# Row sums of squares on TensorE: one 128 by 128 identity per step, or two 64 by 64 identities on the diagonal of the array

## The chip, the core and the metric

The kernel runs on one core of a Trainium2 chip. The core has TensorE (matmuls; PE in the profile, its weight loads PEld), VectorE (DVE), ScalarE (ACT), GpSimd (POOL), SyncE (SP, which only issues DMAs here), an on-chip memory SBUF with 128 partitions, and PSUM, the accumulators that TensorE writes, eight banks in each partition. The metric is the time of one execution on the device in microseconds. Three runs of the kernel before gave 193.05, 191.87 and 192.48 us; the median is 192.48.

## The reference

Cosine-similarity attention for 8 batches of 12 heads, 512 positions, 64 numbers per position:

```python
Q_norm = Q / (np.linalg.norm(Q, axis=-1, keepdims=True) + 1e-10)
K_norm = K / (np.linalg.norm(K, axis=-1, keepdims=True) + 1e-10)
scores = np.einsum('bhqd,bhkd->bhqk', Q_norm, K_norm) / tau          # tau = 0.1
weights = np.exp(scores - np.max(scores, axis=-1, keepdims=True))
weights = weights / (np.sum(weights, axis=-1, keepdims=True) + 1e-10)
return np.einsum('bhqk,bhkd->bhqd', weights, V).astype(np.float32)
```

For each of the 96 heads: a norm for each of 512 rows of Q and of K, 512 by 512 scores, their exponentials, and the weighted sum of V.

## The kernel before

The heads are worked through in 48 pairs, s = 0 to 47. A pair goes through these steps; the names in brackets are those of the program's own order tables.

- **Load** (LD, LV; line 429 and 432): Q and K of a pair into `qk`, V into `vf`.
- **Squares** (SQ, line 250): POOL squares Q and K of the pair into `sq`, 128 partitions of 16 rows of 64 numbers, in bf16.
- **Sums of squares** (SSQ, lines 266 to 271): each of the 16 rows has 64 numbers to be added up. TensorE does the first part. Eight matmuls with the identity matrix `ident` as stationary operand each read 16 rows by 8 numbers (128 columns) and are accumulated in the same 128 columns of PSUM, so that 64 numbers of a row become 8. The changed lines are these. The result lies in bank "x" (and in banks "o1" and "o0" for pairs 1 and 2).
- **Reduce** (RED, line 276): DVE adds up the remaining 8.
- **Norms** (NEW, lines 390 to 402): DVE works out 1/sqrt in a few Newton steps, for groups of one or two pairs.
- **Scale** (SCL, line 296): DVE scales Q, POOL scales K, into `qn`.
- **Transpose** (TR, line 484): 16 matmuls for a pair, each on 64 of the 128 rows of the array (the two halves in turn, written to two banks of PSUM), and a DVE copy (EVA, line 490) into `qt`. For seven pairs K goes through a DMA instead.
- **Scores** (SCO, line 512): four chunks for each pair. A chunk is two matmuls, one for each head, on 64 rows of the array each, 512 columns, into two banks of `scps`. There are two such pairs of banks, used in turn, so a chunk may start when the exponentials of the chunk two before it have been read.
- **Exponentials** (EXP, line 527): ACT reads a chunk, 128 by 1024, and writes `et`. There are 184 such instructions on line 527 and a few others at both ends.
- **Weighted sums** (PV, line 543): 32 matmuls for a pair, each on all 128 rows and columns of the array, 65 columns wide, in eight pieces of four.
- **Normalise and store** (RCP line 557, NRM line 559, ST line 563).

The order of the work is a table written out by hand for each engine (`ORDER`); an engine runs its list in order and waits on semaphores where an operation needs another's result. In TensorE's list each SSQ stands between two other operations. Of the 47 SSQs, 29 stand between two SCOs; 9 come after a PV and before an SCO, 4 after an SCO and before a PV, 2 between two PVs, 2 between an SCO and a TR, 1 between a TR and an SCO. So an SSQ touches a PV on 9 + 4 + 2 x 2 = 17 sides. (One of the two transposes beside an SSQ, that of pair 1 on line 301, uses all 128 rows and columns too; it runs at 11.5 us, before the steady part.)

On the array's shapes, as the profile's rows write them: `64*128` is a matmul on 64 rows and 128 columns of the array (SCO, TR), `128*128` one on the whole array (SSQ, PV), and `128*64` one on 64 columns only (the 16 transposes of pair 0, line 333).

Of the kernel before, what the change touches and what calls it, by code (L numbers as in the profile page):

```python
# [124 lines left out]
def bass_cosine_similarity_attention_kernel(  # L125
# [16 lines left out]
    R_QK, R_V, R_SQ, R_QN, R_QT, R_ET, R_O = 18, 6, 6, 5, 5, 3, 8  # L142
# [3 lines left out]
    def sb(name, shape, dt):  # L146
        return nc.alloc_sbuf_tensor(name, shape, dt)
# [4 lines left out]
    sq = [sb(f"sq{i}", [128, 16, DIM], bf16) for i in range(R_SQ)]  # L152
# [13 lines left out]
    ident = sb("ident", [128, 128], bf16)  # L166
# [49 lines left out]
    def scored(s):  # L216
# [9 lines left out]
        out=ident[:, :], in_=ones[:, :], pattern=[[1, 128]], base=0, channel_multiplier=-1,  # L226
# [26 lines left out]
    def sums(s, dst, free):  # L253

        sqs = [k for k in (("SQ", s, 0), ("SQ", s, 1)) if k in P.ops]
        if s in DIRECT:
            for w in range(2):
                P.add(("RED", s, w), "dve", [sqs[min(w, len(sqs) - 1)], *free],
                      lambda e, w=w: e.tensor_reduce(
                          out=dst(w), in_=sq[s % R_SQ][:, 8 * w : 8 * w + 8, :], axis=AX.X, op=ALU.add))  # L260
            return

        bank = {1: "o1", 2: "o0"}.get(s, "x") if LOGS > 2 or s < 2 else "x"
        ps = {"o0": o_ps[:, 0], "o1": o_ps[:, 1], "x": x_ps}[bank]

        def ssq(e):
            for k in range(8):
                last = e.matmul(  # L268
                    out=ps[:, 0:128], lhsT=ident[:, :], rhs=sq[s % R_SQ][:, :, 8 * k : 8 * k + 8],
                    start=(k == 0), stop=(k == 7))  # L270
            return last

        after = {"o1": [("warm", WARM - 1), ("SCL", 0, 0, 0), ("SCL", 0, 1, 0)], "o0": [("EVA", 0, 1, h) for h in range(2)], "x": []}
        P.add(("SSQ", s), "pe", sqs + ["eye"] + after[bank], ssq, take=[bank], until=("RED", s, 0))
        P.add(("RED", s, 0), "dve", [("SSQ", s), *free],
              lambda e: e.tensor_reduce(  # L276
                  out=dst(None), in_=ps[:, 0:128].rearrange("p (w g e) -> p w g e", w=2, e=8),
                  axis=AX.X, op=ALU.add))
# [550 lines left out]
```

## Time and profile before

| what | value |
|---|---|
| median of three runs | 192.48 us |
| the profiled execution | 192.64 us |
| its span, first to last instruction | 190.9 us |
| ACT busy | 181.9 us (95% of the span) |
| PE busy | 172.5 us (90%) |
| POOL busy | 160.2 us (84%) |
| DVE busy | 145.2 us (76%) |
| SSQ matmuls (line 268) | 376, 29.0 us busy, 220 ns each |
| granted TensorE clock | full speed in all 40 slices |

Busy time of PE is the time in which at least one matmul is under way by the trace, whose ends are modelled. Matmuls overlap: one of line 268 is shown with 220 ns, but eight of them together take 0.62 us. In a row of the timeline the first number is the start, the second the time from the first start to the last end of the instructions that the row joins, "x8" their number, and the bracket at the end the idle time of the engine just before, with what ended it.

### The profile page before, as it was taken

Reading aid. Unit: us, or ns where it says so; the run is one execution under the profiler, and the core shown is the slowest. Engines: PE = TensorE matmul, PEld = TensorE weight load, DVE = VectorE, ACT = ScalarE, POOL = GpSimd, SP = SyncE. Lnnn points to the kernel's source line nnn. Section 1 sums busy time; section 2 is a strip of 40 time slices with the busy share of each in tenths; the row PEclk is TensorE's granted clock in tenths of the full one; section 3 lists DMA queues with packets and bytes.
Section 4 is the critical chain, followed back from the end, with each engine's and each line's share of the span. In section 5 each row is a group of like instructions: output and inputs, shape, how many; then the busy total and the mean of one; then the engine's idle time right before and its main releaser. Section 6 shows DMA issues by size and latency. Waiting matters only on the chain.

```text
span 190.9 us, 7237 instructions
## 1 busy us (share of the span) xinstructions
PE 172.5 (90%) x3023; PEld 110.4 (58%) x3023; DVE 145.2 (76%) x451; ACT 181.9 (95%) x209; POOL 160.2 (84%) x147
## 2 busy tenths in 40 slices
PE   7789898998899999999999899989989999998883
PEld 5446565655555666566566566655656666654542
DVE  1889898968976986688876878868678878696624
ACT  4589999999999999999999999999999999999992
POOL 1399999999999999999999999898998999276000
PEclk9999999999999999999999999999999999999999
DMA  5999899999999999999799999999956929677043
GB/s 155 317 355 350 280 298 307 307 225 361 350 359 267 263 358 372 328 191 349 256 320 280 325 321 379 339 261 317 367 207 212 228 92 283 189 213 173 28 140 115
DMA packets 56257, 51.73 MB, mean 271 GB/s; under 512 B 6944, under 2 KB 56224, under 8 KB 56224
## 3 DMA queue, kind: packets, MB, share of 16 engines
q1 hardware_dynamic: 55792, 50.93, 88.3%
q8 instruction: 24, 0.39, 0.8%
q10 hardware_dynamic: 432, 0.33, 0.6%
q14 instruction: 9, 0.07, 0.1%
HBM read 37.75 MB, written 12.58 MB: 264 GB/s over the span
## 4 chain that ended last, share of the span: by engine, by line
ACT 78%; DVE 6%; PE 6%; POOL 5%; DMA 3%; issue 1%; SPq 0%; DVEq 0%
ACT et L527 76%; DMA qk<-in_Q_dram 3%; POOL sq L250 3%; PE scps L512 2%; DVE qn L296 2%; PE bps L543 2%; POOL qn L296 1%; ACT et L364 1%; DVE qt L490 1%; PE bps L268 1%; POOL vb L532 1%; ACT et L523 1%; DVE nps L276 1%; PE bps L484 0%; SPq L315 0%
## 5 line engine op out<-in xcount | busy, mean ns | idle before, releaser
L527 ACT ACTIVATE et<-scps 128x1024 bf16<-128x1024 f32 x184 | 169.7, 1069 | 0.4
L250 POOL TENSOR_TENSOR sq<-qk 128x1024 bf16<-128x1024 f32 (+2 forms) x48 | 87.4, 1833 | 7.1 <-DMA qk<-in_Q_dram 6.6
L512 PE MATMUL scps<-qt 64*128 64x512 bf16 x376 | 74.1, 385 | 8.3 <-ACT et L527 6.7
L543 PE MATMUL bps<-vb,et 128*128 128x65 bf16 x1504 | 69.4, 194 | 1.0 <-issue 0.3
L543 PEld LDWEIGHTS bps<-vb,et 128*128 128x128 bf16 x1504 | 53.6, 98 | 26.7 <-issue 18.4
L296 POOL TENSOR_TENSOR qn<-qk,rk 128x512 bf16<-128x512 f32 x44 | 45.5, 1044 | 8.7 <-DVE rk L398 8.5
L490 DVE COPY qt<-bps 128x1024 bf16<-128x1024 bf16 (+1 forms) x46 | 29.9, 649 | 13.2 <-PE bps L484 12.8
L296 DVE TENSOR_TENSOR qn<-qk,nps 128x512 bf16<-128x512 f32 x50 | 33.4, 679 | 0.9 <-ACT nps L286 0.6
L559 DVE TENSOR_TENSOR ob<-bps,rd 128x512 f32<-128x512 f32 x47 | 32.5, 691 | 1.3
L512 PEld LDWEIGHTS scps<-qt 64*128 64x128 bf16 x376 | 18.3, 93 | 25.4 <-ACT et L527 13.7
L268 PE MATMUL bps<-sq,ident 128*128 128x128 bf16 x376 | 29.0, 220 | 0.9 <-DVE sq L250 0.5
L532 POOL TENSOR_SCALAR vb<-vf 128x512 bf16<-128x512 f32 x48 | 29.5, 627 | 0.0
L268 PEld LDWEIGHTS bps<-sq,ident 128*128 128x128 bf16 x376 | 21.3, 97 | 9.3 <-issue 6.6
L557 DVE RECIPROCAL rd<-bps 128x8 f32<-128x8 f32 x47 | 9.6, 205 | 17.9 <-PE bps L543 17.3
L484 PE MATMUL bps<-ident,qn 64*128 64x64 bf16 x680 | 17.9, 191 | 3.2 <-DVE nps L276 0.9
L484 PEld LDWEIGHTS bps<-ident,qn 64*128 64x128 bf16 x680 | 13.5, 94 | 10.2 <-DVE nps L276 2.9
L276 DVE TENSOR_REDUCE nps<-bps 128x16 f32<-128x128 f32 x45 | 13.2, 293 | 1.8 <-PE bps L268 1.8
L394 DVE SCALAR_TENSOR_TENSOR nps<-nps,ys 128x32 f32<-128x32 f32 (+1 forms) x48 | 9.3, 194 | 1.2
L390 DVE TENSOR_TENSOR nps<-nps,ys 128x32 f32<-128x32 f32 (+1 forms) x48 | 9.2, 192 | 0.8
L237 PE MATMUL scps<-warm_in 128*128 128x256 bf16 x23 | 4.5, 377 | 1.1 <-DVE warm_in L232 1.1
L402 DVE TENSOR_SCALAR ys<-nps 128x32 int32<-128x32 int32 (+1 forms) x24 | 4.4, 183 | 0.4
L398 DVE SCALAR_TENSOR_TENSOR nps<-nps,ys 128x16 f32<-128x16 f32 (+1 forms) x25 | 4.3, 175 | 0.4
(43 smaller groups left out, 43.4 us busy)
## 6 DMA issues: line engine op xcount, KB each, us to landing
vf<-in_V_dram SPq DMA_DIRECT2D x48, 256.0 KB, 5.1
qk<-in_Q_dram SPq DMA_DIRECT2D x47, 256.0 KB, 5.4
qk<-in_K_dram SPq DMA_DIRECT2D x47, 256.0 KB, 5.8
out_dram<-ob SPq DMA_DIRECT2D x47, 256.0 KB, 4.6
qk<-in_Q_dram SPq DMA_DIRECT2D x2, 128.0 KB, 2.8
qk<-in_K_dram ACTq DMA_DIRECT2D x2, 128.0 KB, 3.0
out_dram<-ob SPq DMA_DIRECT2D x1, 128.0 KB, 1.7
qt<-qn SPq DMA_TRANSPOSE x7, 4.0
```

The source lines that it names most:

```text
L250: emit = lambda e: e.tensor_tensor(out=b, in0=a, in1=a, op=ALU.mult)
L268: last = e.matmul(out=ps[:, 0:128], lhsT=ident[:, :], rhs=sq[s % R_SQ][:, :, 8 * k : 8 * k + 8], start=(k == 0), stop=(k == 7))
L276: lambda e: e.tensor_reduce(out=dst(None), in_=ps[:, 0:128].rearrange("p (w g e) -> p w g e", w=2, e=8), axis=AX.X, op=ALU.add))
L296: lambda e: e.tensor_tensor(out=o, in0=x, in1=r, op=ALU.mult))
L484: last = e.transpose(t_ps[:, k, b, :], qn[s % R_QN][ks, b // NT, b % NT].rearrange("p h d -> p (h d)"), ident[ks, ks])
L490: lambda e, lo=lo, hi=hi: e.tensor_copy(out=qt[iqt][:, :].rearrange("p w t (k x) -> p k (w t) x", k=2)[:, :, lo:hi], in_=t_ps[:, :, lo:hi]))
L512: last = e.matmul(out=sc_ps[:, 2 * b + k, :], lhsT=qt[iqt][64 * h : 64 * h + 64, 1, n, :], rhs=qt[iqt][64 * h : 64 * h + 64, 0, :, :], sta ...
L527: lambda e, c=c, b=b: e.activation(out=et[iet][:, c, :, :], in_=sc_ps[:, 2 * b : 2 * b + 2, :], func=ACT.Exp, scale=scale, bias=bias))
L532: lambda e: e.tensor_scalar(out=vb[:, iq, :, :, 0:DIM].rearrange("p c h d -> p h c d"), in0=vf[iv][:, :, :].rearrange("p h (c d) -> p h c ...
L543: last = e.matmul(out=o_ps[:, h, 65 * t : 65 * t + 65], lhsT=et[iet][:, c, h, 128 * t : 128 * t + 128], rhs=vb[:, iq, c, h, :], start=(c = ...
L557: lambda e: e.reciprocal(out=rd[io][:, :], in_=grid[:, :, :, DIM]))
L559: lambda e: e.tensor_tensor(out=ob[io][:, :], in0=grid[:, :, :, 0:DIM], in1=rd[io][:, :].unsqueeze(3).to_broadcast([128, 2, NT, DIM]), op= ...
```

## The change

Each of the eight matmuls of an SSQ is replaced by two: one on partitions 0 to 63 with the upper left 64 by 64 block of the identity, one on partitions 64 to 127 with the lower right block. Each streams the same 128 columns as before, from half of the partitions, and writes half of the partitions of the same bank. An SSQ is thus 16 matmuls and 16 weight loads, where it was 8 and 8. All order tables, waits and buffers stay as they are.

```diff
         def ssq(e):
             for k in range(8):
-                last = e.matmul(
-                    out=ps[:, 0:128], lhsT=ident[:, :], rhs=sq[s % R_SQ][:, :, 8 * k : 8 * k + 8],
-                    start=(k == 0), stop=(k == 7))
+                for js in (slice(0, 64), slice(64, 128)):
+                    last = e.matmul(
+                        out=ps[js, 0:128], lhsT=ident[js, js], rhs=sq[s % R_SQ][js, :, 8 * k : 8 * k + 8],
+                        start=(k == 0), stop=(k == 7))
             return last
```

No instruction changes its place. Two pieces of TensorE's list show what is replaced, first where an SSQ stands between two chunks of scores (the list before):

```order
L543 MATMUL bps<-vb,et 128x65 x16
L512 MATMUL scps<-qt 128x512 x2
L268 MATMUL bps<-sq,ident 128x128 x8
L512 MATMUL scps<-qt 128x512 x2
L484 MATMUL bps<-ident,qn 128x64 x16
```

and the same place in the list of the change, whose lines are numbered one higher from here on:

```order
L544 MATMUL bps<-vb,et 128x65 x16
L513 MATMUL scps<-qt 128x512 x2
L269 MATMUL bps<-sq,ident 64x128 x16
L513 MATMUL scps<-qt 128x512 x2
L485 MATMUL bps<-ident,qn 128x64 x16
```

The 8 matmuls with an output of 128 partitions have become 16 with an output of 64; the neighbours are the same.

## The prediction

> **What bounds the kernel now.** First the page's head, the costliest group and the chain that ended last, shared out by engine; then the chain's longest pieces in order of time.
>
> ```profile
> span 190.9 us, 7237 instructions
> PE 172.5 (90%) x3023; PEld 110.4 (58%) x3023; DVE 145.2 (76%) x451; ACT 181.9 (95%) x209; POOL 160.2 (84%) x147
> ...
> ACT 78%; DVE 6%; PE 6%; POOL 5%; DMA 3%; issue 1%; SPq 0%; DVEq 0%
> ...
> L527 ACT ACTIVATE et<-scps 128x1024 bf16<-128x1024 f32 x184 | 169.7, 1069 | 0.4
> ...
> 20.55 0.55 PE bps L268 x8
> ...
> 22.30 0.57 PE bps L268 x8
> ...
> 39.41 0.61 PE bps L268 x8
> ...
> 53.73 82.90 ACT et L527 x90
> 136.64 46.92 ACT et L527 x51
> ```
>
> The exponentials of line 527 are the bound: ACT sat idle before them for 0.4 us in all, and from 53.73 to 183.56 us the chain is ACT alone, 141 exponentials at 0.921 us each. TensorE is 90% busy and is on the chain for 6%, mostly before 54 us; three SSQs are named there. So TensorE is not the bound, but near it. How much room has it? The waits of PE, first for 20 to 54 us, then for 54 to 184 us:
>
> ```profile
> PE bps L484 <- DVE qt L490: 0.6, 1, 0.6
> PE bps L484 <- DVE ys L398: 0.5, 1, 0.5
> PE scps L512 <- ACT et L527: 0.4, 1, 0.4
> PE scps L512 <- POOL vb L532: 0.4, 1, 0.4
> PE bps L543 <- issue: 0.3, 1, 0.3
> ```
>
> ```profile
> PE scps L512 <- ACT et L527: 6.0, 19, 0.5
> ```
>
> Late in the kernel PE catches up with ACT 19 times and then waits 0.32 us on average for a free pair of score banks. Early on it waits 2.2 us in five pieces. Some 8.2 us is what PE has left over.
>
> **The change part by part.** *Streaming.* Today's pace, from the timeline of PE and the rows of the groups:
>
> ```profile
> 40.87 0.39 PE L512 MATMUL scps<-qt 64*128 64x512 bf16 x2
> 41.20 0.62 PE L268 MATMUL bps<-sq,ident 128*128 128x128 bf16 x8
> 41.75 0.39 PE L512 MATMUL scps<-qt 64*128 64x512 bf16 x2
> ...
> L268 PE MATMUL bps<-sq,ident 128*128 128x128 bf16 x376 | 29.0, 220 | 0.9 <-DVE sq L250 0.5
> L512 PE MATMUL scps<-qt 64*128 64x512 bf16 x376 | 74.1, 385 | 8.3 <-ACT et L527 6.7
> L484 PE MATMUL bps<-ident,qn 64*128 64x64 bf16 x680 | 17.9, 191 | 3.2 <-DVE nps L276 0.9
> ```
>
> Eight matmuls of 0.220 us each take 0.62, so one starts (0.62 - 0.22)/7 = 0.057 us after the other. After the change 16 matmuls of the same 128 columns have to go through; each pair must stream side by side, or the SSQ takes twice as long. Do halves of the array stream side by side? Two score matmuls of 0.385 us take 0.39 together, so yes, and the transposes agree:
>
> ```profile
> 23.33 0.41 PE L484 MATMUL bps<-ident,qn 64*128 64x64 bf16 x16 [0.48 <-DVE ys L398]
> 23.56 0.40 PE L512 MATMUL scps<-qt 64*128 64x512 bf16 x2
> ```
>
> (0.41 - 0.19)/15 = 0.015 us between starts, half of the 0.029 that 64 columns need at 0.057 for 128. Those pairs use halves of the rows and all columns and write two PSUM banks; the new ones use a quarter each, on the diagonal, and write two halves of the partitions of one bank. No row shows that. Bounds: 0.057 us per pair (side by side) and 0.114 (one after the other). I take 0.057, since both kinds of half-row pairs run side by side and the new tiles share neither rows nor columns.
>
> *Weight loads.* Sixteen loads of 64 columns replace eight of 128. The nearest rows are those of pair 0's transposes, which use 64 columns of the array:
>
> ```profile
> 7.95 0.63 PE L333 MATMUL bps<-ident,qn 128*64 128x128 bf16 x8
> ...
> 7.95 0.14 PEld L333 LDWEIGHTS bps<-ident,qn 128*64 128x64 bf16 x2 [0.42 <-DVE qn L327]
> ...
> 64.74 0.11 PEld L268 LDWEIGHTS bps<-sq,ident 128*128 128x128 bf16 x2 [0.23 <-issue]
> ...
> L268 PEld LDWEIGHTS bps<-sq,ident 128*128 128x128 bf16 x376 | 21.3, 97 | 9.3 <-issue 6.6
> L333 PEld LDWEIGHTS bps<-ident,qn 128*64 128x64 bf16 x16 | 1.0, 109 | 1.4 <-DVE qn L327 1.3
> ```
>
> Two loads of 0.097 us take 0.11, so the second starts 0.013 us behind the first; of the 64-column kind it is 0.14 - 0.109 = 0.03. The narrower load occupies its path more than twice as long. Still eight matmuls with it take 0.63 us, as the 0.62 above: one load per 0.057 us hides behind the stream. Two per 0.057 us need 0.06, which is about even. Exposed is the start of each SSQ (0.03 + 0.03 - 0.013 = 0.05 at most) and at worst 0.003 for each of eight pairs. Bounds 0.02 to 0.07 us per SSQ; I take 0.04, the middle.
>
> Here a rule speaks against the change. The Trainium skill, "TensorEngine Tiling (Array Packing)", section "Restrictions and Gotchas", says that column tiling excludes Fast Weight Load. By that rule, the 0.03 against 0.013 us agrees; if the second load of each pair were not hidden, the result would be the third rival's instead of the forecast's.
>
> *Borders.* A change of the array's shape costs time on PE:
>
> ```profile
> 47.52 0.30 PE L543 MATMUL bps<-vb,et 128*128 128x65 bf16 x4
> 47.66 0.61 PE L268 MATMUL bps<-sq,ident 128*128 128x128 bf16 x8
> 48.10 0.29 PE L543 MATMUL bps<-vb,et 128*128 128x65 bf16 x4
> ...
> 5.67 0.74 PE L333 MATMUL bps<-ident,qn 128*64 128x128 bf16 x8 [0.63 <-DVE qn L327]
> 6.34 0.61 PE L237 MATMUL scps<-warm_in 128*128 128x256 bf16 x4
> ```
>
> From an SSQ's start to the next operation's it takes 48.10 - 47.66 = 0.44 us where the shape stays, and 41.75 - 41.20 = 0.55 where 128 rows give way to 64. The transposes above keep the shape of the scores: 23.56 - 23.33 = 0.23, no more than eight pairs of 0.029. A change of columns alone shows the same: line 237 starts 0.07 us before the shown end of line 333 (5.67 + 0.74 - 6.34), as the scores do before that of the SSQ (41.20 + 0.62 - 41.75), while 47.66 + 0.61 - 48.10 gives 0.17 within one shape. So any change costs 0.10 us. The new shape, 64 rows by 64 columns, is nobody else's. Sides towards scores and transposes cost 0.10 us before and after; the 17 sides towards a PV cost nothing now and 0.10 us then.
>
> *Sum on TensorE.* 45 SSQs run after 13 us (two earlier ones, off the chain, are left out): 45 x 0.04 = 1.8 us, and 17 x 0.10 = 1.7 us; in all 3.5 us (2.6 to 4.9).
>
> *What of it reaches the end.* By the order, 14 of the SSQs run before 54 us, with 6 of the sides: 0.56 + 0.6 = 1.16 us. The other 31, with 11 sides, add 2.34. After 54 us PE waits for ACT every 130/19 = 6.8 us; between two waits stand 1.6 SSQs, which add 0.12 us to a wait of 0.32. ACT's exponentials hide it, except in long stretches without a wait; I put 0.2 us on the path. Without that cover, all 2.34 would be on it. Before 54 us PE itself is on the chain in places (20.55, 22.30, 39.41), in others POOL is:
>
> ```profile
> 40.99 1.89 POOL sq L250
> ...
> 45.44 3.74 POOL sq L250 x2
> ```
>
> There a later PE costs nothing. Bounds 0.3 us (the three SSQs on the chain, 3 x 0.04, and their two sides towards a PV, 0.2) and 1.16; I take 0.6. Behind a longer SSQ waits RED on DVE, and behind RED, in DVE's list, Newton steps and scalings; for an SSQ itself DVE waits little:
>
> ```profile
> L276 DVE TENSOR_REDUCE nps<-bps 128x16 f32<-128x128 f32 x45 | 13.2, 293 | 1.8 <-PE bps L268 1.8
> ```
>
> 1.8 us of idle time before 45 of them, so most find the SSQ done; what 0.04 to 0.14 us more does there is within the 0.6. The sum: 0.6 + 0.2 = 0.8 us later. The profiled execution took 192.64 us (span 190.9 and 1.74 around it), 0.16 over the median of 192.48, which is nothing beside the runs' spread of 1.2. **Forecast: 192.64 + 0.8 = 193.4 us.** Its own range is 192 to 195, with the upper bounds of both parts and the spread.
>
> **The rivals.**
>
> *One after the other (slower).* If the two tiles of a pair don't stream together, an SSQ takes 16 x 0.057 = 0.91 us, not 0.45. That is 45 x 0.456 = 20.5 us on PE, with 3.5 as above 24.0; minus the 8.2 us of waits, 15.8 us come through: 208.4. It decides as soon as an SSQ grows by more than 8.2/45 = 0.18 us, where PE becomes the bound. For it: the pair writes one bank, and both kinds that run side by side today write two. Against it: the halves of the partitions are disjoint, and so are rows and columns. The same section of the Trainium skill's "TensorEngine Tiling (Array Packing)" says that different row tiles cannot use one PSUM bank at the same time, and leaves it to software to keep them apart; no run here shows it, and a wait made by the chip would give this rival's time. "PSUM — Partial Sum Buffer", section "PSUM bank collisions raise a hardware error", lets different column tiles into one bank on disjoint partitions, which these are.
>
> *No border between shapes of 64 rows (faster).* If only a change of rows costs 0.10 us, 75 sides towards scores and transposes become free: 7.5 us less on PE. But ACT sets the pace:
>
> ```profile
> L527 ACT ACTIVATE et<-scps x184: 1012/1058/1229, 13.5 to 182.5; 128x1024 bf16<-128x1024 f32 x184
> ```
>
> 183 steps in 169.0 us; at the 0.920 us of the last 51 they would take 168.4. So 0.6 us is to be had there, and 0.4 from the two SSQs on the chain at 20.55 and 22.30: 191.6 us. Against it stands the border from line 333 to 237, a change of columns alone.
>
> *Half-hidden loads (slower).* If one 64-column load of each pair is exposed, a pair takes 0.087 us: 45 x 8 x 0.03 = 10.8 us, with the sides 12.5. With all 8.2 us of waits used up, 4.3 come through; with half of them, 8.4. Middle 6.3: 199.0 us. For it: two loads need 0.06 us of the 0.057. Against it: the transposes hide two loads in 0.029 us, though of the quicker kind.
>
> **How the numbers follow.** Forecast 0.60, no border 0.14, one after the other 0.12, half-hidden loads 0.10, anything else 0.04. The runs of this kernel lie within 1.2 us, so 1%, 1.9 us, is about what can be told from no change. Faster by over 1% would need more than ACT leaves: 0.03, out of the second rival. Within 1%: 0.50 of the forecast and 0.11 of the second rival, 0.61. Slower: 0.10 of the forecast (its range ends at 195, and 194.4 is 1%), 0.12, 0.10 and 0.04, 0.36. The range runs from 191.3, below the no-border case, to 199.5, which takes in the middle of the half-hidden loads; left out are the pairs one after the other, the upper half of the loads and the rest, 0.19.
>
> **What would show it.** Pairs side by side: the row of line 269 reads x16 in about 0.62 to 0.69 us in the timeline; one after the other it would be over 1.0, half-hidden loads 0.9. Borders: PV to SSQ and back, as at 47.52, 0.10 us longer each; with free ones, scores follow an SSQ after 0.44 us, not 0.55. Pass-through: PE's waits for ACT after 54 us shrink from 6.0 to some 4 us, and the chain there stays ACT alone with about 0.922 us per exponential; if it names PE in that stretch, the forecast is wrong. It is also wrong if RED makes the scalings late.

## The result, and the profile after

The changed kernel takes 194.79 us (median of 15 runs, 193.62 to 195.91), the kernel before 192.48 us in the runs beside it (15 runs, 191.72 to 194.64). The ratio is 1.0117 with a 95% interval of 1.0091 to 1.0143: **2.25 us slower (1.75 to 2.75)**, just past the 1% that was called measurable. (In some executions of these kernels the records show a lower granted TensorE clock and the time is over 1.5% longer; medians here are over all executions, ratios and differences leave those out.) The forecast was 193.4 us, 0.8 us slower, within a range of 191.3 to 199.5.

First the head of the page after, its instruction queue, the chain by engine, and the groups that answer to those shown of before.

```profile
span 193.6 us, 7989 instructions
PE 176.0 (91%) x3399; PEld 113.0 (58%) x3399; DVE 146.1 (75%) x451; ACT 182.7 (94%) x209; POOL 160.3 (83%) x147
...
q8 instruction: 27, 0.44, 0.9%
...
ACT 68%; PE 18%; DVE 8%; DMA 2%; issue 1%; ACTq 0%; DVEq 0%
...
L528 ACT ACTIVATE et<-scps 128x1024 bf16<-128x1024 f32 x184 | 170.4, 1058 | 1.5 <-PE scps L513 1.1
...
L269 PE MATMUL bps<-sq,ident 64*64 64x128 bf16 x752 | 30.0, 219 | 0.8 <-issue 0.5
...
L269 PEld LDWEIGHTS bps<-sq,ident 64*64 64x64 bf16 x752 | 22.4, 106 | 9.8 <-issue 7.3
...
L277 DVE TENSOR_REDUCE nps<-bps 128x16 f32<-128x128 f32 x45 | 13.2, 293 | 2.8 <-PE bps L269 2.6
```

PE is busy 3.5 us longer. Of that, 1.1 us lie before 13 us (10.9 us where it was 9.8), ahead of the SSQs in question; a program equal to the kernel before (the empty instructions below) has 10.8 there, so they do not belong to the change. The other 2.4 us do. Twice as many SSQ matmuls (752) fill nearly the same time, 30.0 us where it was 29.0, so they do run in pairs. PE's share of the chain has gone from 6% to 18%, and the exponentials, which waited 0.4 us in all, now wait 1.5.

The timeline of PE after shows the pairs and the borders: an SSQ between scores, an SSQ between two PVs, and an SSQ that was interrupted.

```profile
41.15 0.39 PE L513 MATMUL scps<-qt 64*128 64x512 bf16 x2
41.47 0.63 PE L269 MATMUL bps<-sq,ident 64*64 64x128 bf16 x16
42.04 0.39 PE L513 MATMUL scps<-qt 64*128 64x512 bf16 x2
...
47.78 0.30 PE L544 MATMUL bps<-vb,et 128*128 128x65 bf16 x4
48.01 0.63 PE L269 MATMUL bps<-sq,ident 64*64 64x128 bf16 x16
48.57 0.30 PE L544 MATMUL bps<-vb,et 128*128 128x65 bf16 x4
...
139.06 0.35 PE L269 MATMUL bps<-sq,ident 64*64 64x128 bf16 x5
139.96 0.49 PE L269 MATMUL bps<-sq,ident 64*64 64x128 bf16 x11 [0.54 <-issue]
```

Sixteen matmuls take 0.63 us where eight took 0.62. From the SSQ's start to the next start it is 0.57 us (41.47 to 42.04), where it was 0.55. Between two PVs it was 0.14 us from the PV to the SSQ and 0.44 from the SSQ to the next PV; now it is 0.23 and 0.56. In the last two rows the fifth matmul of an SSQ is followed by 0.54 us in which PE waited for nothing that the profile shows.

Where the time reached the end is seen on ACT. The timeline of ACT after, 20 to 190 us, broken where the exponentials had to wait:

```profile
21.80 17.64 ACT L528 ACTIVATE et<-scps 128x1024 bf16<-128x1024 f32 x19 [0.27 <-PE scps L513]
39.66 100.55 ACT L528 ACTIVATE et<-scps 128x1024 bf16<-128x1024 f32 x108 [0.23 <-PE scps L513]
140.82 44.28 ACT L528 ACTIVATE et<-scps 128x1024 bf16<-128x1024 f32 x48 [0.60 <-PE scps L513]
```

The longest wait, 0.60 us at 140.82, is what the interrupted SSQ left. The chain around it, which before was ACT alone from 53.73 us on:

```profile
119.41 0.56 PE bps L269 x16
...
131.56 0.56 PE bps L269 x16
...
139.13 0.28 PE bps L269 x5
139.42 0.54 issue
139.96 0.49 PE bps L269 x11
140.45 0.34 PE scps L513 x2
140.82 13.85 ACT et L528 x15
```

And there is a second place, after the last exponential. Of each of the two kernels: first the last two stores on SP's queue from the timeline (start, time to the last issue's end), then, from their issue to the end of the span, the DMA queues' packets (q8 brings PE's instructions, as its count grows with theirs) and the landing of the 128 KB store. Before, from 187.7 us, with no packet of q8:

```profile
187.77 1.28 SPq L620 DMA_DIRECT2D out_dram<-ob  x2
```

```profile
q1 hardware_dynamic: 560, 0.46, 43.8%
q10 hardware_dynamic: 144, 0.07, 7.2%
q14 instruction: 1, 0.01, 1.0%
...
out_dram<-ob SPq DMA_DIRECT2D x1, 128.0 KB, 1.7
```

After, from 189.3 us:

```profile
189.32 1.83 SPq L621 DMA_DIRECT2D out_dram<-ob  x2
```

```profile
q8 instruction: 1, 0.02, 1.3%
...
out_dram<-ob SPq DMA_DIRECT2D x1, 128.0 KB, 3.3
```

The engines' work ended 1.55 us later (189.32 against 187.77). From there to the end it took 193.6 - 189.32 = 4.3 us, where it had been 190.9 - 187.77 = 3.1. So of the 2.7 us between the two profiled spans, 1.55 came through the exponentials, 0.6 of it at the interruption, and 1.2 came in the last stores, with an instruction packet among them. (The first exponentials ended 0.3 us earlier than before, so from there on the loss is 1.9 us; two executions of equal programs differ by 0.3 us over the same stretch.) The profiled execution after took 195.46 us, 0.67 over the median, so the sizes are those of one rather long execution.

### The profile page after: what moved, and what is told of

Read it like the earlier page. It is cut to its first block, busy times and chain, and to the rows that moved or that the text cites. A ratio compares the mean times of both kernels' runs of the same rounds, so it can differ in the third digit from the quotient of the medians.

```text
span 193.6 us, 7989 instructions
## 1 busy us (share of the span) xinstructions
PE 176.0 (91%) x3399; PEld 113.0 (58%) x3399; DVE 146.1 (75%) x451; ACT 182.7 (94%) x209; POOL 160.3 (83%) x147
## 4 chain that ended last, share of the span: by engine, by line
ACT 68%; PE 18%; DVE 8%; DMA 2%; issue 1%; ACTq 0%; DVEq 0%
ACT et L528 67%; PE bps L544 7%; PE scps L513 6%; PE bps L269 3%; DVE qn L297 2%; DVE ob L560 2%; DMA qk<-in_K_dram 2%; PE bps L485 1%; DVE qt L491 1%; PE bps L334 1%; DVE nps L277 1%; ACT et L524 1%; DVE rd L558 1%; PE scps L360 0%; PE scps L237 0%
## 5 line engine op out<-in xcount | busy, mean ns | idle before, releaser
L269 PE MATMUL bps<-sq,ident 64*64 64x128 bf16 x752 | 30.0, 219 | 0.8 <-issue 0.5
L269 PEld LDWEIGHTS bps<-sq,ident 64*64 64x64 bf16 x752 | 22.4, 106 | 9.8 <-issue 7.3
L237 PE MATMUL scps<-warm_in 128*128 128x256 bf16 x23 | 5.0, 404 | 1.1 <-DVE warm_in L232 1.1
L399 DVE SCALAR_TENSOR_TENSOR ys<-nps,ys 128x32 f32<-128x32 f32 (+1 forms) x24 | 4.4, 182 | 0.3
```

The lines of the kernel that those rows point to most:

```text
L269: last = e.matmul(out=ps[js, 0:128], lhsT=ident[js, js], rhs=sq[s % R_SQ][js, :, 8 * k : 8 * k + 8], start=(k == 0), stop=(k == 7))
```

## The experiments

Three theories stood first. **Array time**: the change keeps the array longer, and part of that reaches the end. **Instructions**: the 752 added instructions of PE cost something by themselves, whatever they compute. **Borders or loads**: one kind of added array time counts more than the other. A later one, of the **last packet**, came out of all the profiles side by side and is told at the end of this section. The added array time is given as measured from individual rows: 0.11 us for each side towards a PV, 0.011 for an SSQ between scores, so 2.25 us for the change (17 sides at 0.09 to 0.12, 45 SSQs at about 0.01). That this is also the number of the measured loss is a coincidence: the one is time on PE, the other time at the end.

**Parts of the change.** The first two runs split its SSQs: those that touch no PV, and those that do.

```diff
+            halves = (slice(0, 64), slice(64, 128)) if s > 2 and s not in BESIDE_PV else (slice(0, 128),)
...
+                for js in halves:
...
+BESIDE_PV = {4, 6, 11, 14, 15, 17, 25, 29, 30, 31, 34, 36, 39, 41, 43}
```

> The tile pairs in only those 30 SSQs that touch no PV (pairs 1 and 2 keep whole identities too). TensorE gets 30 x 0.015 = 0.45 us more, no new border of shapes, and 480 more instructions. Theory 'borders' (the 17 new changes of shape, 0.10 us each, are the loss, and nearly all of it comes through): +0 to +0.5 us against the kernel before. Theory 'instructions' (752 more instructions, whose supply stalls TensorE now and then, are the loss): 480/752 of 2.3 us, +1.5 us. Theory 'cover' (ACT hides what TensorE loses, as forecast, and the rest is chance): +0.2 us, and so in the second run below.

Measured: 193.57 us (192.96 for the nine executions that the ratio takes in) where before takes 192.2, ratio 1.0041 (1.0009 to 1.0073), so +0.8 us (0.2 to 1.4). It adds 0.33 us of array time and 480 instructions.

The other 15 SSQs alone (`if s in BESIDE_PV`):

> The tile pairs in only those 15 SSQs that touch a PV, 17 sides. TensorE gets 17 x 0.10 + 15 x 0.015 = 1.9 us more, with 240 more instructions. Theory 'borders': +1.3 to +2.0 us against the kernel before. Theory 'instructions': 240/752 of 2.3 us, +0.7. Theory 'cover': +0.5.

Measured: 194.13 us, 1.0094 (1.006 to 1.0129), +1.8 us (1.2 to 2.5), with 1.93 us of array time and 240 instructions. The parts add up to 2.6 us, the whole to 2.25: within their intervals. By the middle values the sides towards PV hold most of the loss; the two intervals overlap.

**The borders without the instructions.** Only one of the eight matmuls of those 15 SSQs becomes a tile pair: the last, or the first where a PV follows. In 13 of them this is the end away from the PV, beside the scores, so that the new change of shape lies inside the SSQ; between two PVs it makes two. That gives 17 more changes of shape, as before, with 30 added instructions.

```diff
+                pair = s in BESIDE_PV and k == (0 if s in PV_BEHIND else 7)
+                for js in (slice(0, 64), slice(64, 128)) if pair else (slice(0, 128),):
...
+PV_BEHIND = {4, 6, 11, 31}
```

> Whole identities everywhere, but in the 15 SSQs that touch a PV one matmul of the eight (the last, or the first where the PV stands behind) is a pair of tiles: the same 17 changes of shape more as in the second run, 1.7 us of array time, with 30 more instructions instead of 240. Theory 'borders': +1.3 to +2.0 us, as the second run. Theory 'instructions' with a third of array time coming through: 0.35 x 1.7 = +0.6.

Measured: 193.14 where before takes 192.09, 1.0046 (1.0027 to 1.0065), +0.9 us (0.5 to 1.25) for 1.97 us of array time. The same array time as the run before it, and by the middle values half the loss: 45% of it reached the end (26 to 63% by the interval).

**Array time with hardly an instruction.** A ninth matmul in every SSQ, which writes what the next one overwrites:

```diff
-            for k in range(8):
+            for k in [0] * 1 + list(range(8)):
```

> The kernel before with a ninth matmul in each SSQ (the first one twice, the second time overwriting): 0.057 us more in each SSQ, 45 x 0.057 = 2.6 us on TensorE after 13 us, no new border, 94 more instructions. It measures what comes through of an even load of that size. Theory 'borders' (comes through nearly in full): +1.8 to +2.6 us. Theory 'instructions': +0.3. Theory 'cover': +0.6.

Measured: 193.37, 1.0053 (1.0029 to 1.0078), +1.0 us (0.6 to 1.5) for 2.5 us of array time, that is 40% (22 to 60%). With three more instead (`[0] * 3`):

> The kernel before with three more matmuls in each SSQ: 45 x 0.171 = 7.7 us of array time, 282 more instructions. If a third of array time comes through, +2.7 and some 0.4 for the instructions, +3.1 us. If the 8.2 us of TensorE's waits were all usable, +0.4. If everything comes through, +7.7.

Measured: 196.7, 1.0216 (1.018 to 1.0251), +4.15 us (3.5 to 4.8) for 7.5 us, 55%. The chain by engine on the page of this kernel, and then its waits of PE:

```profile
ACT 47%; PE 37%; DVE 8%; DMA 3%; issue 2%; SPq 1%; DVEq 0%
```

```profile
PE scps L512 <- ACT et L527: 4.0, 14, 0.5
...
PE bps L543 <- issue: 1.1, 1, 1.1
```

After 7.5 us more, PE still waits 4.0 us for ACT. The 8.2 us of waits that stood in the prediction as room are thus no common store: half of an added microsecond passes while other waits remain unused, as it seems because they lie elsewhere. Two kinds of array time, matmuls here and borders above, pass about the same share, 40 to 45% by the middle values. For the change's 2.25 us that makes 0.9 to 1.0 us (0.5 to 1.4 with the intervals), not 2.25.

**Instructions without the array time.** Whole identities, but each matmul split into two of 64 columns:

```diff
+                for c in range(2):
+                    last = e.matmul(
+                        out=ps[:, 64 * c : 64 * c + 64], lhsT=ident[:, :],
+                        rhs=sq[s % R_SQ][:, 8 * c : 8 * c + 8, 8 * k : 8 * k + 8],
...
```

> Whole identities, but each of the eight matmuls split into two of 64 columns: as many instructions as in the change (752 more), the shape of the whole array as before, so no new border. By the 0.029 us per 64 columns TensorE gets about 0.02 us more per SSQ, 0.9 in all. Theory 'borders': +0.3 to +0.9 us against the kernel before. Theory 'instructions': the whole +2.3. Theory 'cover': +0.2.

Measured: 193.56, 1.0073 (1.004 to 1.0105), +1.4 us (0.8 to 2.0) with 752 instructions and 0.9 us of array time, of which 0.4 would pass. About 1 us is left over, and the profile of this kernel shows no stall like that at 139.42. The same 752 in another place, with each score matmul of 512 columns split into two of 256:

```diff
+                for q in range(2):
...
-                            rhs=qt[iqt][64 * h : 64 * h + 64, 0, :, :], start=True, stop=True)
+                            rhs=qt[iqt][64 * h : 64 * h + 64, 0, 2 * q : 2 * q + 2, :], start=True, stop=True)
```

> Whole identities as before; each later score matmul of 512 columns is split into two of 256. That is 752 more instructions, the number that the change adds, at a place where they add little array time (some 0.002 to 0.004 us for each of 188 chunks, 0.6 in all). Theory 'supply' (four tenths of the array time comes through, and 752 more instructions cost 1.1 us of their own because they have to be fetched): 0.2 + 1.1 = +1.3 us against the kernel before. Theory 'array time alone': 0.2 to 0.6.

Measured: 194.31 where before takes 192.05, 1.0108 (1.007 to 1.0146), +2.1 us (1.3 to 2.8), for 0.4 us of array time. Five of its nine runs had a mean granted TensorE clock of 0.978 to 0.994 and four one of 0.997 to 1.0; the median of those four is 193.4, so 1.3 us of the loss stand without the clock. (The change itself shows no such link: its seven runs at a granted clock of 1.0 have a median of 194.89, the five at 0.994 to 0.996 one of 194.79.) The waits of this kernel, and its chain from 99 to 122 us:

```profile
ACT et L528 <- PE scps L513: 1.5, 2, 1.1
...
PE scps L513 <- issue: 1.2, 1, 1.2
```

```profile
99.82 0.32 PE scps L513 x3
100.14 1.19 issue
101.32 0.28 PE scps L513
101.60 0.02 issue
101.62 21.22 ACT et L528 x23
```

PE stands still for 1.19 us between the third and the fourth matmul of one chunk, as in the change at 139.42. The individual packets of the trace put one of the instruction queue at 99.1 to 100.0 us, just ahead of it; in the change one ended 0.9 us ahead of the stall, and in the run with three more matmuls 0.3 us ahead of its 1.1. The run with the tiles one after the other (below) has one of 0.9 at 40.4 us, 0.6 us behind the end of a packet. A list that ran dry and waited for its next piece would stand still until a packet has arrived; these stalls begin after one has, and no other packet is under way during them. So their cause is open, and no run isolates it. They do not go with the number of instructions alone: the profile of the split sums, with the same 752, has no such stall, nor have those with 480, 240 and 30 added, and that of before has one of 0.3, 1.0 us behind a packet.

Two runs were to add instructions alone. The first put four empty instructions after each chunk of scores:

```diff
+                for _ in range(4):
+                    e.nop(nofuse=True)
```

> The kernel before with four empty instructions behind each of the 188 later chunks of scores on TensorE's list: 752 more instructions, as many as the change adds, that compute nothing and stand where the array is still streaming 512 columns. Theory 'instructions' (supplying 752 more instructions costs about 1.1 us, whatever they do): +0.8 to +1.5 us against the kernel before. Theory 'borders' (only array time counts): 0, within 0.4.

Measured: 192.23, 1.0008 (0.9984 to 1.0032). But the page still has 7237 instructions and 24 packets of q8: the empty instructions never reached the chip, and the run tells only that equal programs measure equal. The second put four increments of a semaphore there that nobody waits for (`e.sem_inc(P.pad, 1)`):

> Whole identities; four increments of a semaphore that nobody waits for stand behind each of the 188 later chunks of scores: 752 more instructions that the array never sees. They take the sequencer 0.05 us each, 0.2 us while the array streams a chunk for 0.216. Theory 'supply': +1.1 us against the kernel before, and 27 packets of instructions instead of 24. Theory 'array time alone': 0, or as much as the trace shows the array to be held up by the sequencer.

Measured: 207.87, 1.0738 (1.0675 to 1.0801), +14 us, where the instructions by themselves were put at +1.1. From its waits of PE:

```profile
PE bps L484 <- issue: 2.4, 5, 1.1
...
PE bps L546 <- issue: 1.4, 6, 0.6
```

The increments hold up PE in its list at 14/752 = 0.02 us each, so the run says nothing of instructions that are only fetched.

**The rival that pairs run one after the other**, as a kernel: all eight upper tiles first, then the eight lower.

```diff
-            for k in range(8):
-                for js in (slice(0, 64), slice(64, 128)):
+            for js in (slice(0, 64), slice(64, 128)):
+                for k in range(8):
```

(against the change)

> The tile pairs of the change in another order: eight matmuls of the upper tile, then eight of the lower one, so that no two neighbours are different tiles. If tiles side by side are what keeps an SSQ at 0.45 us, it takes 0.9 here and the kernel comes to about 206 to 209 us (the first rival's price). If the chip overlaps them anyway: as the change, 194.8.

Measured: 201.31 us at a granted clock of 1.0, 9.2 more than before, and 205.8 at 0.979, the profiled one. At 100 us, where its clock was full, the timeline of PE shows

```profile
100.97 0.88 PE L269 MATMUL bps<-sq,ident 64*64 64x128 bf16 x16
101.78 0.39 PE L513 MATMUL scps<-qt 64*128 64x512 bf16 x2
```

0.81 us per SSQ where the change has 0.57, and not the 0.9 of the rival. The individual rows of an SSQ show why: eight matmuls start at 0, 0.080, 0.136 and so on to 0.415 us, and among them a second train of eight from 0.253 over 0.333 and 0.389 to 0.668, each at a step of 0.056 us. The rows do not say which tile they are on, but two such trains are what two tiles would give that overlap for some 0.2 us although they are not neighbours in the list. So the order of the list decides how much of the two tiles runs side by side: all of it in the change, less than half here.

**Fewer, wider matmuls.** Four of 256 columns instead of eight of 128 with whole identities save 376 instructions, and RED adds 16 partial sums instead of 8:

```diff
+            for k in range(4):
...
+                        out=ps[js, 0:256], lhsT=ident[js, js], rhs=sq[s % R_SQ][js, :, 16 * k : 16 * k + 16],
+                        start=(k == 0), stop=(k == 3))
...
+                  out=dst(None), in_=ps[:, 0:256].rearrange("p (w g e) -> p w g e", w=2, e=16),
```

> Whole identities, but four matmuls of 256 columns per SSQ instead of eight of 128, and the reduction on DVE adds up 16 numbers instead of 8: the same array time, 376 instructions fewer, some 0.13 us more in each of 45 reductions on DVE (256 columns for 128 at the 1.04 ns that 0.293 us for 128 columns allows at most). Theory 'supply': -0.5 us from the instructions, and what DVE's 6 us cost, 0 to +1. Theory 'array time alone': 0 to +1.

Measured: 195.74, 1.0167 (1.0131 to 1.0204), +3.2 us, where at most +1 was expected. And the same with tile pairs, which has as many instructions as before:

> The same with the change's tile pairs: four pairs of 64 by 64 tiles of 256 columns. The borders of the change, and just as many instructions as the kernel before. Against the run just before this one, theory 'supply': four tenths of 2.2 us of array time and 376 instructions, 0.9 + 0.55 = +1.5 us; theory 'array time alone' (all of it comes through): +2.2 us. Against the change itself, 'supply' gives -1.1 us and DVE's cost.

Measured: 195.87, 1.0185 (1.0155 to 1.0216), +3.55 us. The pairs cost 0.35 us here, with an interval of about -0.6 to 1.2, so they decide nothing. The page of the first of the two suggests why:

```profile
ACT 41%; DVE 23%; PE 17%; POOL 8%; DMA 5%; issue 3%; SPq 0%; ACTq 0%; DVEq 0%
...
L277 DVE TENSOR_REDUCE nps<-bps 128x16 f32<-128x256 f32 x45 | 19.1, 425 | 1.9 <-PE bps L269 1.9
```

RED takes 425 ns where it took 293, 5.9 us more in all; DVE stands on the chain for 23%, where it was 6%, and may cover what PE does beside it. No version tried beat the kernel before.

**The last packet.** The runs with many instructions lose about 1 us that array time does not explain, and at first a price per instruction seemed to fit: 1.1 us for 752 agrees with the change and with both splits. But by it the 15 SSQs beside PV, with 240 instructions, should lose 0.8 + 0.35 = 1.15 us, and they lost 1.8 (1.2 to 2.5), which is only just out of its reach, while the 30 quiet SSQs fit it (0.15 + 0.7 = 0.85 us, against 0.8). So the times alone do not rule out a price per instruction. The ends of the profiles tell it otherwise. Here are the same two views for the run with 15 SSQs beside PV, from 187.5 us on:

```profile
187.52 1.50 SPq L622 DMA_DIRECT2D out_dram<-ob  x2
```

```profile
q8 instruction: 1, 0.02, 1.6%
...
out_dram<-ob SPq DMA_DIRECT2D x1, 128.0 KB, 2.9
```

and of the run with the 30 quiet SSQs, from 187.8 us, with twice the added instructions and no packet of q8 there:

```profile
187.81 1.28 SPq L622 DMA_DIRECT2D out_dram<-ob  x2
```

```profile
q1 hardware_dynamic: 560, 0.46, 44.8%
q10 hardware_dynamic: 144, 0.07, 7.4%
q14 instruction: 1, 0.01, 1.1%
...
out_dram<-ob SPq DMA_DIRECT2D x1, 128.0 KB, 1.7
```

In both, the engines were done at about the time of before (187.77); one lost 0.8 us behind that point and the other nothing. Over all fourteen profiles, with the packet's place taken from its individual row:

| kernel | PE instructions added | packet near the last stores, us from their issue | issue of the last stores, us | from there to the end, us |
|---|---|---|---|---|
| before | 0 | -1.2 to -0.1 | 187.77 | 3.1 |
| empty instructions | 0 | -1.4 to -0.2 | 187.29 | 3.1 |
| four pairs of 256 | 0 | -1.2 to -0.3 | 190.92 | 3.1 |
| border alone | 30 | -2.1 to -0.9 | 188.47 | 3.1 |
| ninth matmul | 94 | -2.2 to -1.3 | 188.40 | 3.1 |
| three more | 282 | -1.5 to -0.2 | 192.81 | 3.15 |
| four of 256 | -376 | -5.5 to -4.5 | 191.34 | 3.1 |
| 30 quiet | 480 | 4.2 to 5.5 | 187.81 | 3.1 |
| 15 beside PV | 240 | 0.1 to 1.1 | 187.52 | 3.9 |
| split sums | 752 | -0.3 to 1.3 | 187.81 | 4.0 |
| split scores | 752 | -0.4 to 1.0 | 188.74 | 3.7 |
| one after the other | 752 | -0.3 to 1.0 | 199.98 | 4.0 |
| increments | 752 | -0.3 to 0.7 | 199.60 | 3.5 |
| the change | 752 | 0.5 to 1.4 | 189.32 | 4.3 |

In the six profiles where a packet lies among the last stores, the end takes 0.4 to 1.2 us longer; in the eight where it lies before or after them it takes 3.1 us, whatever the kernel. The counts tell why these six: 24 packets (0.39 MB) carry PE's 6119 instructions (3023 matmuls, as many loads, 73 others) and 27 carry 6871, so a packet of 16 KB holds about 255. Adding 752 is three packets less some 13 instructions, adding 240 one packet less some 15: all six have the last piece of the list fetched that much nearer to the end than before, which takes it from just ahead of the last stores to among them. Adding 480 moves it by some 30 and past the end.

The packet seems to hold one of the 16 DMA engines that the stores need, and the individual rows of the stores' packets (q1) bear it out. Each store ends in 16 packets of 4 bytes. In the change, of the store before the last two (issued at 188.48) and of the first of the last two (189.32), 15 of the 16 have landed by 190.28 and 190.69, and the sixteenth only at 191.80 and 192.14. In between, from 190.74, just as the instruction packet ends (190.75), 24 packets of 1 KB follow one behind the other until 192.14. So one share in sixteen of these stores came behind the instruction packet. Before, all 16 land within 0.2 us (188.57 to 188.73, 188.99 to 189.15). The split sums show the same: 15 by 188.76, the sixteenth at 190.11, behind an instruction packet that ended at 189.08. The pattern comes from comparing the profiles afterwards. How often it strikes in executions without a profile is not known, and the 30 quiet SSQs, whose profile is free of it, still lost 0.8 us over all their executions, more than the packet and the array time explain. The run that would test it was not tried: the change with one SSQ left as it was has 16 instructions fewer, should free the last stores, and should gain back 0.4 to 1.2 us.

## Why the prediction came out as it did

**The bound** was named rightly: ACT's exponentials still hold 68% of the chain.

**Streaming, side by side**: right. The sixteen take 0.63 us, within the 0.62 to 0.69 announced; the two of a pair start 3 ns apart and the pairs 56 ns, by the individual rows. The rival of pairs one after the other is ruled out. Its price, 0.91 us per SSQ and 208.4 us, was not reached by the kernel that puts the tiles one after the other in the list (0.81 and 201.3), which still overlaps them in part. On the Trainium skill, "TensorEngine Tiling (Array Packing)", section "Restrictions and Gotchas", and its sentence on row tiles and one PSUM bank: two row tiles that write different partitions of one bank start 3 ns apart in this trace, so it does not hold for such pairs.

**Weight loads**: a cost was right, its mechanism was not, and it was too large. A load of 64 columns is slower (106 ns for 97), but the two loads of a pair do not queue up 0.03 us apart: by the individual rows they start 3 ns apart, as the matmuls do. What is left is the start of the SSQ, where the second pair's loads come 0.028 us behind the first, against 0.015 before (after scores). An SSQ between scores grew by 0.011 us, where 0.04 was taken (0.02 to 0.07). Over 45 SSQs that is 0.5 us instead of 1.8; the half-hidden loads are ruled out.

**Borders**: right. 0.10 us for every change of shape, and the 17 sides towards PV cost 0.09 to 0.12 us each; an SSQ is still 0.57 us ahead of scores, so the rival without a border between 64-row shapes is ruled out too. (Its 75 sides should be 73: 45 SSQs have 90, less 17. Nothing hangs on it.)

**Sum on PE**: 2.25 us, not 3.5 (2.6 to 4.9), because of the loads.

**What of it reaches the end** is the step that failed, in two ways. First the share and the place. The prediction let 0.8 of 3.5 us through, 23%, where the runs with matmuls or borders alone pass 40 to 45%; 23% lies at the lower edge of their intervals. This error and that of the loads nearly cancel, as 0.9 to 1.0 us of 2.25 pass. The place is the clearer miss: 0.6 us was put before 54 us and 0.2 behind. By the individual rows of both traces the 8th to 24th exponentials of line 528 (527 before) ended 0.3 us earlier than before, the 48th, at 58.5 us, at the same time, the 100th 0.28 later, the 120th 0.71 and the 144th, after the interruption, 1.41. So 0.3 us were lost up to 58 us and 1.6 behind. The stall of 0.3 us that before itself has at 52 us lies in the first stretch; against the equal program without it (the empty instructions) it is 0.65 us up to the 48th and 1.5 behind. The first part thus agrees with the forecast. The second failed: 0.7 us of it is the interruption, and 0.8 to 0.9 us are left where 0.2 was put. The prediction spread the late SSQs evenly over PE's waits, 1.6 of them between two waits, and had these waits shrink from 6.0 to some 4 us. They shrank far less. The waits of PE after, from 54 to 187 us, begin with:

```profile
PE scps L513 <- ACT et L528: 5.3, 19, 0.5
```

The chain at 119.41 to 140.45 shows that stretches without a wait are long enough for PE to fall behind ACT. "If it names PE in that stretch, the forecast is wrong" applied. The other sign, that RED makes the scalings late, did not show on DVE: RED waited 1.0 us more for the SSQs in all (2.8 for 1.8), DVE's scalings 0.9 us as before.

Second, a missing term. The sum counted what the added instructions do in the array, not that they must be fetched. Of the 2.25 us lost, 0.9 to 1.0 is array time. In the profiled execution the last stores took 1.2 us longer with a packet among them, and 0.4 to 1.2 in the six profiles of that kind. Together 1.3 to 2.2 us, against 1.75 to 2.75 measured. What remains is of the size of the stall at 139.42, which cost the exponentials 0.6 us in that execution and need not occur in all. That the packet causes the late landing is read from the traces and not tested by a run; what causes the stall is open.

The range held the time, since it reached far up for other reasons (half-hidden loads). The forecast's own range of 192 to 195 held it too, by 0.2 us, though it allowed nothing for the last stores or a stall; that is luck. The likeliest outcome, within 1%, was missed by 0.3 us.

## What to carry to other kernels

An operation split into more instructions is worth costing a second time as a list that is fetched: count the packets of the instruction queue, and see what transfer the last of them meets, above all the final stores. An engine that was 90% busy beside the bound passed on 40 to 55% of what was added to it here, although it had waits left; measure that share with one spare operation per burst. Tile pairs on the diagonal pay nothing here where the whole array already streamed the same columns in the same time, and each border towards another shape costs 0.10 us.

## What the hardware showed that was not expected

- The end of the kernel takes 3.1 us from the issue of the last stores in eight profiles and 3.5 to 4.3 in the six that have a 16 KB instruction packet among them.
- PE stood still for 0.54 us (the change), 1.1 us (three more matmuls), 1.19 us (split scores) and 0.9 us (tiles one after the other), waiting for nothing that the profile shows; each time from 0.1 to 0.9 us after such a packet had ended. Why is open.
- 752 semaphore increments in PE's list cost 14 us, though nobody waited for them.
- Sixteen matmuls on 64 by 64 tiles took 0.81 us when eight on one quarter of the array stood ahead of eight on the other, and 0.57 when they alternated. In the first order, too, the two seem to overlap for some 0.2 us.
- The weight loads of two tiles on the diagonal start 3 ns apart, as their matmuls do.
